# Two-step means and gated weight splits in a two-layer encoder kernel

## The chip, the core and the metric

The kernel runs on one core of a Trainium2 chip. Five engines work side by side, each through its own queue in order: TensorE (PE in the profile; PEld is its weight load), VectorE (DVE), ScalarE (ACT), GpSimd (POOL), and SyncE (SP), which here issues loads. Data comes from memory by DMA into SBUF; TensorE writes into the banks of PSUM. The metric is the time of one execution on the device in microseconds (us), lower is better.

## What is computed

Two layers of an encoder over 256 tokens of width 1024, with a memory of 256 tokens. Cut to what matters here:

```python
for l in range(2):
    x = x + 0.5 * swiglu(rms_norm(x, ffn1_norm[l]), ffn1_w_in[l], ffn1_w_out[l])   # D_FF = 2816
    z = rms_norm(x, mix_norm[l]) @ w_mix_in[l]
    o = [mla_mixer(z..), swa_mixer(z..), na_mixer(z..)]        # three groups of attention heads
    x = x + concat(rms_norm of each group of o) @ w_mix_out[l]
    x = x + mem_xattn(rms_norm(x, mem_norm_x[l]), mem, ...)
    x = x + 0.5 * swiglu(rms_norm(x, ffn2_norm[l]), ffn2_w_in[l], ffn2_w_out[l])
    x = rms_norm(x, block_norm[l])

def mem_xattn(h, mem, mem_g, w_q, w_kv, q_gain, k_gain, w_o):
    m = rms_norm(mem, mem_g)
    q = rms_norm((h @ w_q).reshape(B, S, 4, 64), q_gain)
    kv = (m @ w_kv).reshape(B, M, 2, 4, 64)
    k = rms_norm(kv[:, :, 0], k_gain);  v = kv[:, :, 1]
    p = softmax(einsum('bshd,bmhd->bhsm', q, k) * 64**-0.5)
    return einsum('bhsm,bmhd->bshd', p, v).reshape(B, S, 256) @ w_o
```

All of it is in float32. `rms_norm` divides by the root of the mean square over the last axis, and `swiglu` is `(silu(g) * u) @ w_out` with `g, u` the halves of `x @ w_in`.

## The kernel before

`x` lies transposed, as eight tiles of 128 features x 256 tokens. Each product of two float32 matrices is made of three matmuls (`mm3`, L171): both sides are split into a rounded high part and the rest, and high x high, high x low and low x high are added up in PSUM.

**Weights.** They come as 332 pieces of 128 x 1024 or less in the order of use (`weight_plan`, L43). For each piece `emit_split` (L131) issues a load on SP's queue into one of four `raw` buffers, a cast to `whi` on ScalarE (L142) and a subtraction to `wlo` on VectorE (L145). So the load of a piece waits for the split of the piece four ahead of it. `piece` (L156) hands out a piece and has those up to three ahead split (`ahead`, L151). In layer 0 pieces 94 and 95 are `wq`, 96 and 97 the values' weights `kvv`, 98 and 99 `wo`, 100 and following `f2i`.

**Order.** The engines' queues are filled by a scheduler that reorders within data dependences by a model of time; `tc.issue_after(x)` keeps an instruction behind `x`, and `state["gate"]` (L144) does that for the subtraction of a split.

**Norms.** `Normed` (L187) makes high and low parts of `x` times a gain, squares, and running sums of the squares; the factor 1/rms is multiplied in later. `stats` (L250) takes the mean by two small matmuls per sum of squares (one for each 128 tokens; the trace records each twice), adds EPS on VectorE, and has GpSimd take the root (`rsqrt`, L177). The norm at the end of layer 0 and the one that opens layer 1 are taken together: that `Normed` (`n10`) has two kinds of sums (`pre`), and `stats` writes four columns of `n10ps` behind each other. Other names: `n0`, `n20`, `n21` open the FFNs `f01` (layer 0, first), `f02`, `f12`; `nx0`, `nx1` the mixers; `nm0`, `nm1` the memory attentions.

**FFN** (`ffn`, L295). 22 columns j of the hidden layer, each a gate and an up part of eight `mm3`; columns 0 and 1 are computed together from four banks (`f11s` in `f11`), those from 2 on as `f11i`. `stats` is called behind column 2, `bcast` (L277, `n10pb`: two transposes of the factor) in column 3, and from there VectorE and ScalarE evacuate the columns. Then eight output tiles of 22 `mm3` (`f11o`). `mc` is the first product of the mixer behind it.

**Memory attention** (`mem_attn`, L905). TensorE computes the queries `me0wq` (`formb`), then values of the memory (`kv0kvv`, 16 `mm3` in stretches of 4, 9 and 3) to fill the time in which the head factors are made: `nm0ps` to `nm0m` (mean), `me0e`, `me0m` (with the heads' squares `me0hs`), the root `me0f` on GpSimd, and `me0qn`, the normed queries. `me0pt` transposes them; ScalarE and VectorE copy a half each to `me0qT`. `attend` (L498) goes through four heads: `sc` scores, `ng` the negated maximum, `p` the exponential, `pt` and `pT` its transpose and copies, `pv` values; `finish` divides by the sum (`rc`, `me0o`). `me0ot` transposes the result, and `project` multiplies it with `wo` and adds it into `x` (`gx`), from which `n20h` and `n20l` are made for `f02s`. In layer 1 the names have a 1 (`me1qn`).

## Time and profile before

| | us |
|---|---|
| median of 3 runs (lowest, highest) | 1054.6 (1054.37, 1056.76) |
| the profiled execution | 1054.34 |
| its span, first to last instruction | 1052.6 |
| TensorE busy | 1026.4 |
| VectorE, ScalarE, GpSimd busy | 725.8, 556.7, 68.7 |

The profile is of one execution. Its times are in us from the first instruction. Ends of matmuls are modelled, so that the pace of matmuls is read from their starts or from their count in a window. In a timeline a row may stand for several instructions (x8), and idle time ahead of it stands in brackets with what ended it.

### The profile page before, as it was taken

The numbers are of one execution on the slowest core, as the hardware profiler recorded it, in microseconds if no ns is written. First come the engines' busy times: TensorE is split into PE (matmuls) and PEld (weight loads), VectorE is DVE, ScalarE is ACT, GpSimd is POOL, SyncE is SP. The second block draws the span as 40 slices with busy tenths as digits, with TensorE's granted clock in tenths as the row PEclk, the third lists the DMA queues.
The fourth block names the chain that finished last, engine by engine and source line by source line (L and its number), as shares of the span: only waits on it lengthen the run. The fifth ranks groups of instructions, "written<-read, shape, count | busy, mean of one in ns | idle before, by whom it ended". The sixth has DMA issues, their size and how long they took to land.

```text
span 1052.6 us, 20896 instructions
## 1 busy us (share of the span) xinstructions
PE 1026.4 (98%) x8480; PEld 1005.2 (95%) x8480; DVE 725.8 (69%) x1299; ACT 556.7 (53%) x928; POOL 68.7 (7%) x72
## 2 busy tenths in 40 slices
PE   9999999999997999999999999999999799999996
PEld 8999999988996999999999999999889789999996
DVE  7866677788775876666757666667886768877651
ACT  6745555666553665555545444546674546544541
POOL 1000000361001000000000000002500000000000
PEclk9999999999998999999999999999999999999998
DMA  8866665654022565566555555656631307766641
GB/s 274 281 199 199 187 211 183 198 192 150 17 97 89 197 223 196 189 197 197 190 185 191 181 185 191 205 171 174 226 108 46 124 33 259 206 196 196 190 137 41
DMA packets 54673, 181.79 MB, mean 173 GB/s; under 512 B 6064, under 2 KB 9264, under 8 KB 54576
## 3 DMA queue, kind: packets, MB, share of 16 engines
q1 hardware_dynamic: 53856, 179.33, 53.5%
q8 instruction: 66, 1.08, 0.4%
q10 hardware_dynamic: 720, 1.12, 0.3%
q14 instruction: 31, 0.25, 0.1%
HBM read 179.38 MB, written 1.05 MB: 171 GB/s over the span
## 4 chain that ended last, share of the span: by engine, by line
PE 92%; DVE 2%; POOL 1%; DMA 1%; ACT 1%; issue 1%; SPq 0%; POOLq 0%; DVEq 0%; ACTq 0%
PE f11i L174 4%; PE f11i L172 4%; PE f11i L173 4%; PE f12i L172 3%; PE f01i L173 3%; PE f02i L172 3%; PE f02i L173 3%; PE f01i L172 3%; PE f02i L174 3%; PE f12i L174 3%; PE f12i L173 3%; PE f01i L174 3%; PE f11o L174 2%; PE f11o L172 2%; PE f11o L173 2%; PE f12o L172 2%
## 5 line engine op out<-in xcount | busy, mean ns | idle before, releaser
L145 DVE TENSOR_TENSOR wlo<-raw,whi 128x1024 fp32r<-128x1024 f32 (+4 forms) x337 | 402.6, 1200 | 201.4 <-ACT whi L142 200.0
L142 ACT CAST whi<-raw 128x1024 fp32r<-128x1024 f32 (+4 forms) x337 | 343.8, 1024 | 342.0 <-issue 98.3
L172 PE MATMUL f11i<-n10h,whi 128*128 128x256 f32 x320 | 90.1, 282 | 0.0
L173 PE MATMUL f11i<-n10l,whi 128*128 128x256 f32 x320 | 89.8, 281 | 0.0
L174 PE MATMUL f11i<-n10h,wlo 128*128 128x256 f32 x320 | 89.8, 281 | 0.0
L172 PE MATMUL f01i<-n0h,whi 128*128 128x256 f32 x320 | 88.6, 277 | 0.0
L172 PE MATMUL f02i<-n20h,whi 128*128 128x256 f32 x320 | 88.5, 276 | 0.0
L172 PE MATMUL f12i<-n21h,whi 128*128 128x256 f32 x320 | 88.5, 276 | 0.0
L174 PE MATMUL f02i<-n20h,wlo 128*128 128x256 f32 x320 | 88.5, 276 | 0.0
L174 PE MATMUL f12i<-n21h,wlo 128*128 128x256 f32 x320 | 88.5, 276 | 0.0
L173 PE MATMUL f01i<-n0l,whi 128*128 128x256 f32 x320 | 88.4, 276 | 0.0
L173 PE MATMUL f02i<-n20l,whi 128*128 128x256 f32 x320 | 88.4, 276 | 0.0
L173 PE MATMUL f12i<-n21l,whi 128*128 128x256 f32 x320 | 88.4, 276 | 0.0
L174 PE MATMUL f01i<-n0h,wlo 128*128 128x256 f32 x320 | 88.2, 276 | 0.0
L173 PEld LDWEIGHTS f11i<-n10l,whi 128*128 128x128 f32 x320 | 61.4, 192 | 0.0
L174 PEld LDWEIGHTS f02i<-n20h,wlo 128*128 128x128 f32 x320 | 60.1, 188 | 0.0
L174 PEld LDWEIGHTS f12i<-n21h,wlo 128*128 128x128 f32 x320 | 60.1, 188 | 0.0
L173 PEld LDWEIGHTS f01i<-n0l,whi 128*128 128x128 f32 x320 | 60.1, 188 | 0.0
L172 PEld LDWEIGHTS f11i<-n10h,whi 128*128 128x128 f32 x320 | 60.1, 188 | 0.0
L173 PEld LDWEIGHTS f02i<-n20l,whi 128*128 128x128 f32 x320 | 60.1, 188 | 0.0
L173 PEld LDWEIGHTS f12i<-n21l,whi 128*128 128x128 f32 x320 | 60.1, 188 | 0.0
L172 PEld LDWEIGHTS f01i<-n0h,whi 128*128 128x128 f32 x320 | 60.1, 188 | 0.0
(1026 smaller groups left out, 2916.7 us busy)
## 6 DMA issues: line engine op xcount, KB each, us to landing
raw<-in_w SPq DMA_DIRECT2D x311, 512.0 KB, 4.3
raw<-in_w SPq DMA_DIRECT2D x12, 384.0 KB, 3.5
raw<-in_w SPq DMA_DIRECT2D x8, 416.0 KB, 3.2
kv0mt<-in_mem SPq DMA_DIRECT2D x8, 128.0 KB, 4.3
kv1mt<-in_mem SPq DMA_DIRECT2D x8, 128.0 KB, 3.4
gx<-in_gx SPq DMA_DIRECT2D x2, 256.0 KB, 6.1
gx<-in_gx ACTq DMA_DIRECT2D x1, 323.0 KB, 3.9
raw<-in_w SPq DMA_DIRECT2D x2, 128.0 KB, 4.0
```

The costliest lines, as they stand in the source:

```text
L142: ins = nc.scalar.copy(hi[:, a:b], r[:, a:b])
L145: sub = nc.vector.tensor_tensor(lo[:, a:b], r[:, a:b], hi[:, a:b].bitcast(F32), ALU.subtract)
L172: nc.tensor.matmul(ps, ah, bh, start=first, stop=False)
L173: nc.tensor.matmul(ps, ah, bl, start=False, stop=False)
L174: return nc.tensor.matmul(ps, al, bh, start=False, stop=last)
```

## The change

`mean(n)` is cut out of `stats`: it takes the mean of one kind of sum, and allocates the PSUM tile and makes `m` with the first. A `Normed` with two kinds has the first mean taken behind column 1 of the FFN and the second with `stats` behind column 2. In the memory attention a limit is set on how many pieces are split: four from the first piece of `wq`. Then `one_piece` admits one piece at a time, at four places, and gates its subtraction behind an instruction of VectorE there: behind `me0m`, behind the half of `me0qT`, and at two steps of `attend` behind the copies `pT` or the maximum. The gate of the next is the low part of the attention's result (`me0ol`).

```diff
-    state = {"split": 0, "cur": 0, "tiles": {}, "gate": None}
+    state = {"split": 0, "cur": 0, "tiles": {}, "gate": None, "limit": len(plan)}
...
     def ahead(n):
-        while state["split"] < min(len(plan), n):
+        while state["split"] < min(state["limit"], n):
...
+        def mean(self, n):
+
+            self.total()
+            if n == 0:
+                self.ps = acc(self.name + "ps")
+            v = self.sums[n]
+            for t in range(2):
...
+            if n == 0:
+                self.m = mp.tile([P, 2], F32, tag="r", name=self.name + "m")
+                nc.vector.tensor_scalar(self.m, self.ps[:, 0:2], EPS, None, ALU.add)
+
         def stats(self, r=None):
...
+            self.mean(0 if self.pre is None else 1)
...
             held.append((j, pg, pu))
+            if j == 1 and nx.pre is not None:
+                nx.mean(0)
             if j == 2:
                 nx.stats()
...
-                nc.vector.tensor_reduce(ng, sc, AX.X, ALU.max, negate=True)
+                state["place"] = nc.vector.tensor_reduce(ng, sc, AX.X, ALU.max, negate=True)
...
-            nc.vector.tensor_copy(self.pT[:, 1, :], ps[:, T : 2 * T])
+            state["place"] = nc.vector.tensor_copy(self.pT[:, 1, :], ps[:, T : 2 * T])
...
-        nc.vector.scalar_tensor_tensor(t3(m), t3(hs), 1.0 / dim, bc(e, n), ALU.mult, ALU.add)
+        state["place"] = nc.vector.scalar_tensor_tensor(t3(m), t3(hs), 1.0 / dim, bc(e, n), ALU.mult, ALU.add)
...
+    def one_piece():
+
+        state["gate"], state["limit"] = state["place"], state["limit"] + 1
+        ahead(state["limit"])
+        state["gate"] = None
+
     def mem_attn(l, nx, mem, nxt):
         nm = f"me{l}"
+
+        state["limit"] = state["cur"] + 4
         ps = formb(nm, "wq", 256, 4, nx.h, nx.l)
...
             nx.stats()
-            state["gate"] = None
...
         f = head_factors(nm, hs, 4, 64, e)
+
+        one_piece()
...
-        nc.vector.tensor_scalar(qT[:, 1], pt[:, T:], gq, None, ALU.mult)
+        state["place"] = nc.vector.tensor_scalar(qT[:, 1], pt[:, T:], gq, None, ALU.mult)
+        one_piece()
...
-            nc.vector.tensor_tensor(ol[:, c, :], pt[:, 0:T], oh[:, c, :].bitcast(F32), ALU.subtract)
-
-        attend(heads, {AT["wturn0"]: [lambda: out_transposed(0)]}, AT["e1"], AT["e2"])
+            state["gate"] = nc.vector.tensor_tensor(ol[:, c, :], pt[:, 0:T], oh[:, c, :].bitcast(F32), ALU.subtract)
+
+        hooks = {AT["wturn0"]: [lambda: out_transposed(0)]}
+        hooks[3] = hooks[5] = [one_piece]
+        attend(heads, hooks, AT["e1"], AT["e2"])
+        state["limit"] = len(plan)
```

VectorE's queue before, from the split of piece 97 on in layer 0's memory attention (the number behind `wlo` is the piece):

```order
L145 TENSOR_TENSOR wlo97_3999<-raw97_3996,whi97_3998 128x1024
L145 TENSOR_TENSOR wlo98_4029<-raw98_4026,whi98_4028 128x1024
L145 TENSOR_TENSOR wlo99_4059<-raw99_4056,whi99_4058 128x1024
L145 TENSOR_TENSOR wlo100_4065<-raw100_4062,whi100_4064 128x1024
L263 TENSOR_SCALAR nm0m_4084<-nm0ps_4081 128x2
L528 TENSOR_SCALAR me0e_4086<-nm0m_4084 128x2
L145 TENSOR_TENSOR wlo101_4255<-raw101_4252,whi101_4254 128x1024
L522 SCALAR_TENSOR_TENSOR me0m_4095<-me0hs_4088,me0e_4086 128x8
L145 TENSOR_TENSOR wlo102_4299<-raw102_4296,whi102_4298 128x1024
L919 TENSOR_TENSOR me0qn_4099<-me0wq0_3994,me0f_4096 128x256
L919 TENSOR_TENSOR me0qn_4099<-me0wq1_3995,me0f_4096 128x256
L935 TENSOR_SCALAR me0qT_4148<-me0pt_4133,me0gq_4102 128x256
```

and in the changed kernel:

```order
L145 TENSOR_TENSOR wlo97_3999<-raw97_3996,whi97_3998 128x1024
L265 TENSOR_SCALAR nm0m_4066<-nm0ps_4063 128x2
L539 TENSOR_SCALAR me0e_4068<-nm0m_4066 128x2
L533 SCALAR_TENSOR_TENSOR me0m_4077<-me0hs_4070,me0e_4068 128x8
L145 TENSOR_TENSOR wlo98_4084<-raw98_4081,whi98_4083 128x1024
L939 TENSOR_TENSOR me0qn_4087<-me0wq0_3994,me0f_4078 128x256
L939 TENSOR_TENSOR me0qn_4087<-me0wq1_3995,me0f_4078 128x256
L955 TENSOR_SCALAR me0qT_4136<-me0pt_4121,me0gq_4090 128x256
L145 TENSOR_TENSOR wlo99_4142<-raw99_4139,whi99_4141 128x1024
L469 TENSOR_REDUCE me0a00ng_4151<-me0a00sc_4148 128x2
```

The splits of pieces 98 to 102, which stood ahead of `me0qn`, are behind `me0m` (98), behind `me0qT` (99) and further on. VectorE's queue before, in the middle of the attention, from the second head's copies to the division:

```order
L484 COPY me0a01pT_4199<-me0a01pt_4194 128x256
L485 COPY me0a01pT_4199<-me0a01pt_4194 128x256
L484 COPY me0a10pT_4207<-me0a10pt_4202 128x256
L485 COPY me0a10pT_4207<-me0a10pt_4202 128x256
L484 COPY me0a11pT_4220<-me0a11pt_4215 128x256
L485 COPY me0a11pT_4220<-me0a11pt_4215 128x256
L432 RECIPROCAL me0a0rc_4227<-me0a0pv_4210 128x4
L434 TENSOR_TENSOR me0o_4151<-me0a0pv_4210,me0a0rc_4227 128x2x64 x2
L432 RECIPROCAL me0a1rc_4240<-me0a1pv_4231 128x4
```

and in the changed kernel:

```order
L495 COPY me0a01pT_4193<-me0a01pt_4188 128x256
L496 COPY me0a01pT_4193<-me0a01pt_4188 128x256
L145 TENSOR_TENSOR wlo100_4199<-raw100_4196,whi100_4198 128x1024
L495 COPY me0a10pT_4207<-me0a10pt_4202 128x256
L496 COPY me0a10pT_4207<-me0a10pt_4202 128x256
L495 COPY me0a11pT_4220<-me0a11pt_4215 128x256
L496 COPY me0a11pT_4220<-me0a11pt_4215 128x256
L145 TENSOR_TENSOR wlo101_4234<-raw101_4231,whi101_4233 128x1024
L443 RECIPROCAL me0a0rc_4227<-me0a0pv_4210 128x4
L443 RECIPROCAL me0a1rc_4246<-me0a1pv_4237 128x4
L445 TENSOR_TENSOR me0o_4145<-me0a0pv_4210,me0a0rc_4227 128x2x64 x2
L445 TENSOR_TENSOR me0o_4145<-me0a1pv_4237,me0a1rc_4246 128x2x64 x2
```

The splits of pieces 100 and 101 stand between the copies and ahead of the reciprocals, and the second reciprocal is ahead of the first product. The split of piece 102 comes behind the two `me0ol`, ahead of the first sum into `gx`. Layer 1 has the same order. TensorE's queue before, at the mean matmuls of `n10` behind column 2 of `f11`:

```order
L172 MATMUL f11i2_6796<-n10h_5912,whi171_6738 128x256
L173 MATMUL f11i2_6796<-n10l_5913,whi171_6738 128x256
L174 MATMUL f11i2_6796<-n10h_5912,wlo171_6739 128x256
L258 MATMUL n10ps_6861<-cmean_87,n10s_6282 128x1 x2
L258 MATMUL n10ps_6861<-cmean_87,n10s_6286 128x1 x2
L172 MATMUL f11i3_6874<-n10h_5912,whi172_6768 128x256
L173 MATMUL f11i3_6874<-n10l_5913,whi172_6768 128x256
L174 MATMUL f11i3_6874<-n10h_5912,wlo172_6769 128x256
```

and in the changed kernel, at the first of two places, behind column 1:

```order
L336 MATMUL f11s2_6674<-n10l_5913,whi169_6678 128x256
L336 MATMUL f11s3_6675<-n10l_5913,whi169_6678 128x256
L259 MATMUL n10ps_6800<-cmean_87,n10s_6282 128x1 x2
L172 MATMUL f11i2_6805<-n10h_5912,whi170_6708 128x256
L173 MATMUL f11i2_6805<-n10l_5913,whi170_6708 128x256
L174 MATMUL f11i2_6805<-n10h_5912,wlo170_6709 128x256
```

and at the second, behind column 2:

```order
L172 MATMUL f11i2_6805<-n10h_5912,whi171_6738 128x256
L173 MATMUL f11i2_6805<-n10l_5913,whi171_6738 128x256
L174 MATMUL f11i2_6805<-n10h_5912,wlo171_6739 128x256
L259 MATMUL n10ps_6800<-cmean_87,n10s_6286 128x1 x2
L172 MATMUL f11i3_6874<-n10h_5912,whi172_6768 128x256
L173 MATMUL f11i3_6874<-n10l_5913,whi172_6768 128x256
L174 MATMUL f11i3_6874<-n10h_5912,wlo172_6769 128x256
```

One group of four small matmuls became two groups of two, 48 matmuls of column 2 apart. The two transposes `n10pb0` stand two matmuls earlier than before, inside a weight piece's triple. ScalarE's queue has one change for each layer: the cast of piece 102 stands behind `me0qT` instead of ahead of it. The queues of GpSimd and SP keep their order.

## Rows read from the trace of the kernel before

**Rows 1.** The page, part 1: busy time, share of the span, instructions.

```profile
PE 1026.4 (98%) x8480; PEld 1005.2 (95%) x8480; DVE 725.8 (69%) x1299; ACT 556.7 (53%) x928; POOL 68.7 (7%) x72
```

**Rows 2.** Waits of TensorE (PE): engine, line, waited for: total us, times, longest.

```profile
PE me0pt L930 <- DVE me0qn L919: 7.5, 1, 7.5
PE me1pt L930 <- DVE me1qn L919: 6.0, 1, 6.0
```

**Rows 3.** Timeline of VectorE (DVE), layer 0's memory attention: start, us, instruction [idle before].

```profile
310.32 4.62 DVE L145 TENSOR_TENSOR wlo<-raw,whi 128x1024 fp32r<-128x1024 f32 x4
314.87 0.15 DVE L263 TENSOR_SCALAR nm0m<-nm0ps 128x2 f32<-128x2 f32 x1
318.31 0.16 DVE L522 SCALAR_TENSOR_TENSOR me0m<-me0hs,me0e 128x8 f32<-128x8 f32 x1
321.23 0.76 DVE L919 TENSOR_TENSOR me0qn<-me0wq,me0f 128x256 f32<-128x256 f32 x2 [1.56 <-POOL me0f L178]
326.77 0.69 DVE L458 TENSOR_REDUCE me0a00ng<-me0a00sc 128x2 f32<-128x512 f32 x1 [2.73 <-PE me0a01sc L455]
```

**Rows 4.** Timeline of TensorE, the mean matmuls of layer 0's memory attention.

```profile
310.46 0.61 PE L258 MATMUL nm0ps<-cmean,nm0s 128*128 128x1 f32 x4
```

**Rows 5.** Timeline of ScalarE (ACT), the cast of piece 101, and layer 1's.

```profile
316.09 1.04 ACT L142 CAST whi<-raw 128x1024 fp32r<-128x1024 f32 x1 [1.57 <-DMA raw<-in_w]
...
837.35 1.04 ACT L142 CAST whi<-raw 128x1024 fp32r<-128x1024 f32 x1 [0.87 <-DMA raw<-in_w]
```

**Rows 6.** Timeline of GpSimd (POOL), the root of the head factors, both layers.

```profile
318.55 2.65 POOL L178 TENSOR_TENSOR me0f<-me0m,nhalf 128x8 f32<-128x8 f32 x1 [33.35 <-DVE me0m L522]
...
839.82 1.67 POOL L178 TENSOR_TENSOR me1f<-me1m,nhalf 128x8 f32<-128x8 f32 x1 [32.75 <-DVE me1m L522]
```

**Rows 7.** Table by window, behind the wait: busy (count) by engine, granted clock, DMA.

```profile
core 0: us, PE busy (x) PEld busy (x) DVE busy (x) ACT busy (x) POOL busy (x), PEclk, DMA share, GB/s
321.70:324.80 3.10, 3.09 (x14) 2.71 (x14) 0.77 (x2) 0.47 (x1) 0.00 (x0) 0.50 0.47 178
```

**Rows 8.** The same table, five windows of the FFNs `f01`, `f02`, `f11`.

```profile
12.50:20.50 8.00, 8.00 (x70) 8.00 (x69) 7.30 (x14) 5.77 (x10) 0.00 (x0) 1.00 0.86 285
345.00:355.00 10.00, 10.00 (x87) 10.00 (x86) 9.38 (x17) 6.53 (x13) 0.00 (x0) 1.00 0.36 114
370.00:470.00 100.00, 100.00 (x884) 100.00 (x884) 68.02 (x100) 52.05 (x78) 0.00 (x0) 1.00 0.61 201
526.00:536.00 10.00, 10.00 (x91) 10.00 (x90) 4.91 (x4) 3.44 (x5) 0.00 (x0) 1.00 0.62 204
550.00:650.00 100.00, 100.00 (x851) 100.00 (x851) 67.53 (x103) 48.94 (x74) 0.00 (x0) 1.00 0.57 187
```

**Rows 9.** Timeline of VectorE, layer 1's memory attention.

```profile
832.30 4.62 DVE L145 TENSOR_TENSOR wlo<-raw,whi 128x1024 fp32r<-128x1024 f32 x4
841.74 0.75 DVE L919 TENSOR_TENSOR me1qn<-me1wq,me1f 128x256 f32<-128x256 f32 x2
846.46 0.69 DVE L458 TENSOR_REDUCE me1a00ng<-me1a00sc 128x2 f32<-128x512 f32 x1 [1.92 <-PE me1a01sc L455]
852.64 0.18 DVE L432 RECIPROCAL me1a0rc<-me1a0pv 128x4 f32<-128x4 f32 x1
852.93 0.49 DVE L434 TENSOR_TENSOR me1o<-me1a0pv,me1a0rc 128x128 f32<-128x128 f32 x2
```

**Rows 10.** Timeline of TensorE, layer 1's memory attention.

```profile
845.30 0.48 PE L455 MATMUL me1a00sc<-memkT,me1qT 64*128 64x256 f32 x1
854.23 0.39 PE L949 MATMUL me1ot<-ident,me1o 128*128 128x128 f32 x2
855.13 0.62 PE L172 MATMUL me1wo<-me1oh,whi 128*128 128x256 f32 x3 [0.52 <-ACT me1oh L950]
```

**Rows 11.** Timeline of TensorE, start of layer 0's second FFN (`f02s`).

```profile
342.44 1.07 PE L327 MATMUL f02s<-n20h,wlo 128*128 128x256 f32 x8
343.35 1.12 PE L327 MATMUL f02s<-n20l,whi 128*128 128x256 f32 x8
```

More of the change, by code (lines that the diff above doesn't have):

```diff
@@ L248, in total @@
             return self.sums[-1][0][-1]
-        def stats(self, r=None):
-            self.total()
-            ps = acc(self.name + "ps")
-            for n, v in enumerate(self.sums):
-                for t in range(2):
-                    s = slice(t * P, (t + 1) * P)
-                    for m, q in enumerate(v):
-                        nc.tensor.matmul(
-                            ps[:, 2 * n + t : 2 * n + t + 1], q[0][:, s], cmean[:, 0:1],
-                            start=m == 0, stop=m == len(v) - 1,
-                        )
-            self.m = mp.tile([P, 2], F32, tag="r", name=self.name + "m")
-            nc.vector.tensor_scalar(self.m, ps[:, 0:2], EPS, None, ALU.add)
+        def mean(self, n):
[4 more added lines that the diff above has]
+            for t in range(2):
+                s = slice(t * P, (t + 1) * P)
+                for m, q in enumerate(v):
+                    nc.tensor.matmul(
+                        self.ps[:, 2 * n + t : 2 * n + t + 1], q[0][:, s], cmean[:, 0:1],
+                        start=m == 0, stop=m == len(v) - 1,
+                    )
+            if n == 0:
+                self.m = mp.tile([P, 2], F32, tag="r", name=self.name + "m")
+                nc.vector.tensor_scalar(self.m, self.ps[:, 0:2], EPS, None, ALU.add)
+        def stats(self, r=None):
+            self.mean(0 if self.pre is None else 1)
             if self.factor:
@@ L271, in stats @@
             m2 = small(2, self.name + "m2")
-            nc.vector.scalar_tensor_tensor(m2, self.m, EPS, ps[:, 2:4], ALU.mult, ALU.add)
+            nc.vector.scalar_tensor_tensor(m2, self.m, EPS, self.ps[:, 2:4], ALU.mult, ALU.add)
             self.r0 = mp.tile([P, 2], F32, tag="r", name=self.name + "r0")
```

## The prediction

> **What bounds the kernel now.** I first read the busy line of the page: TensorE (PE) is busy for 98% of the span [rows 1]. So nothing gains but a shorter wait of TensorE, or matmuls that follow each other faster. The waits view names only two waits of TensorE above 1.5 us, one in the memory attention of each layer, 7.5 and 6.0 us, both for `qn`, the normed queries that VectorE (DVE) writes [rows 2]. Then the timeline of DVE shows why `qn` is late [rows 3]. The mean `nm0ps` is on TensorE at 310.46 and takes 0.61 us [rows 4], so DVE could read it at 311.1. But four splits of weight pieces (`wlo`, 4.62 us) stand ahead of its first reader, which starts at 314.87; the fifth split waits for ScalarE, which waits for a load [rows 5], and `me0m` comes only at 318.31. GpSimd's root follows for 2.65 us [rows 6] and `qn` starts at 321.23. During the wait the clock fell: right behind it the granted clock is 0.50, the lower level of 1.2 GHz [rows 7].
>
> The second thing is the pace of the matmuls in the FFNs. All have 256 columns. I take the pace as (window + 0.28 us, since matmuls stick out at its edges) / count. In `f02i` it is 100.28/884 = 113.4 ns, in `f11i` 100.28/851 = 117.8 ns, both at a granted clock of 1.00 [rows 8]. So there is a quick and a slow pace, 4.4 ns apart. The switches stand at the mean matmuls: `f01` is slow ahead of `n0ps` (8.28/70 = 118 ns), `f02` slow ahead of `n20ps` (10.28/87 = 118) and quick behind it, `f11` quick ahead of `n10ps` (10.28/91 = 113) and slow behind it [rows 8]; `f12` repeats `f02`.
>
> **The change: the gates of the memory attention.** In layer 0 one split (piece 97) now stands ahead of `nm0m`, instead of four. It starts at 310.32 as before [rows 3]; with 4.62/4 = 1.15 us each, `nm0m` can start at 311.5. `me0e` and `me0m` follow directly, about 0.18 us later each (an estimate from the 0.15 to 0.17 us that such instructions take [rows 3]), so `me0m` is at 311.85. The root starts 0.24 us behind it as now (318.31 to 318.55 [rows 3, 6]), takes 2.65 us, and `qn` starts at 311.85 + 0.24 + 2.65 + 0.03 = 314.77 instead of 321.23: **6.46 us** earlier. The split of piece 98, gated behind `me0m`, lies under the root. TensorE's work ends at about 321.7 - 7.5 = 314.2 and the transposes come 0.48 us behind `qn`, so some 1.0 us of wait stays.
>
> In layer 1 the first split starts at 832.30 [rows 9]; `nm1m` 833.45, `me1m` 833.8, root 834.05 to 835.72 (1.67 us [rows 6]), `qn` 835.75 instead of 841.74: **5.99 us**, and the wait all but goes (842.2 - 6.0 = 836.2 is where TensorE's work ends).
>
> Behind the transposes the clock matters. After a wait of 1.0 us or none I take it to stay at 1.00; now that stretch runs at 0.50 [rows 7]. What that gives is bounded by nothing and by half of the 3.1 us stretch plus, in layer 0, the scores. It isn't all to be had: ScalarE has the cast of piece 101 ahead of its copy `qT`, and that cast waits for a load whose issue hangs on the first split, which does not move. It starts at 316.09 and takes 1.04 us [rows 5], so `qT` is at 317.1 and its end at 317.6. From the first score to the first reduction it takes 846.46 - 845.30 = 1.16 us at full clock [rows 9, 10]; the split of piece 99, now ahead of that reduction, adds some 0.3. So the reduction is at about 319.0, where the 6.46 us alone would give 326.77 - 6.46 = 320.3: **1.3 us** more in layer 0 (0 to 2.0). In layer 1 the cast runs from 837.35 to 838.4, `qT` to 838.9, the reduction at 840.0 to 840.4 against 846.46 - 5.99 = 840.5 [rows 5, 9]: **0.3 us** (0 to 1.0).
>
> The price: pieces 100 and 101 are split in the middle of the attention, the one ahead of the last two heads' copies, the other ahead of the reciprocal. Two splits are 2.3 us; DVE waits little there (some 0.15 us), so the reciprocal goes from 852.64 to about 854.8. The second reciprocal is now ahead of the first product too (0.2 us), so the product that starts at 852.93 ends near 855.7, and the transposes at 854.23 become 855.7 [rows 9, 10]. The projection behind them (855.13) is **1.5 us** later, in each layer; bounds 0.3 (they fit into gaps) and 2.3. The split of piece 102, between `ol` and the first sum into `x`, costs nothing: TensorE has the whole projection there, and if that cover failed it would be 1.15 us. Loads for later pieces are issued later on SP's queue, since a load waits for the split of the piece four ahead of it; with 24 matmuls a piece, piece 103 is needed 72 x 113.4 ns = 8 us after `f02s` starts, so I price that at nothing, and at 1 us if one piece is late.
>
> Sum: layer 0 -6.46 - 1.3 + 1.5 = -6.3; layer 1 -5.99 - 0.3 + 1.5 = -4.8. Together **-11.1 us**.
>
> **The change: the means in two steps.** The work is the same, four mean matmuls, which the trace records as x8 in one group; now two groups of x4. No engine is waited for there in either place, and the root behind them isn't on the path. What can change is the pace. Three groups of x4 came in at the slow pace and left at the quick one (`n0ps`, `n20ps`, and `n21ps`, which repeats `n20ps`). The new first group comes in at the quick pace; what it leaves is not shown, since the only x4 groups that came in quick (`nm0ps`, `nm1ps`) did so behind a wait of their own. But if it leaves the quick pace, the second one meets the same case and leaves it too; if it leaves the slow one, the second is the case seen three times, slow to quick. Either way `f11` runs quick from there, if the pair of transposes `n10pb` keeps the pace, as the pairs in the other three FFNs do. Matmuls from there to the end of `mc` in layer 1: 19 columns x 48 = 912, `f11o` 8 x 66 = 528, `mc` 72, together 1512 x 4.4 ns = 6.7 us; if column 2 runs slow it costs 48 x 4.4 ns = 0.2. So **-6.4 us**; bounds +0.2 and -6.7.
>
> [...]
>
> **Sum.** The profiled execution took 1054.34 us around its span of 1052.6. 1054.34 - 11.1 - 6.4 = 1036.8. The median shown is 0.26 above the profiled execution: **1037.1 us**. Its own bounds: 1033.5 (1.2 us less for each tail, 0.7 more for each clock term) to 1040.5 (0.8 more for each tail, no clock gain).
>
> **Rivals.** *The pace stays slow* (0.28). The single group of x8 came in quick and left slow, and the pairs `n10pb0` and `n10pb1` left it so; the new `n10pb0` stands inside a weight piece, where the quick FFNs have theirs between two pieces. If the pace belongs to what stands around the matmuls there, the split means bring +0.2: 1037.1 + 6.6 = 1043.7 us. [...]
>
> *DVE and ScalarE take the place of the wait* (0.08): both inserted splits lie fully on the path (+0.8 per layer) and the casts of 1.04 us delay `qT` and the first exponential by one each (+1.04 per layer): +3.7, 1040.8 us.
>
> *The pace turns the wrong way* (0.06), the one that ends slower. `f02s` starts quick and turns slow where it waits for `n20l`: its eight matmuls at 343.35 take 1.12 instead of 1.07 us [rows 11]; only so does `n20ps` come in slow and leave quick. If the moved splits take that wait of 0.05 us away, `f02s` stays quick and `n20ps` may turn it slow, up to the end of `f11s` (912 + 528 + 96 = 1536 matmuls), and likewise `f12` to the end (1440): 2976 x 4.4 ns = 13.1 us, less 1.1 for the quick rest of both `f02s` and `f12s`. `f11` then comes in slow, is quick for one column, and slow again: nothing gained. 1054.6 - 11.1 + 12.0 = 1055.5 us. It decides from the point where `n20l` is in time. Against it: the split of piece 102 ends before the sums into `x`, so the chain from there to `n20l` stays as it is.
>
> *The change doesn't do what it says* (0.02): something else holds `nm0m`, and nothing moves: 1054.6. The order above speaks against it.
>
> **How the numbers follow.** Forecast 0.56, slow pace 0.28, DVE and ScalarE 0.08, wrong way 0.06, nothing 0.02. The range must reach the slow pace at 1043.7 and the low bound of the forecast: 1034.0 to 1044.8. A measurement tells this kernel from no change at about 0.3%, 3.2 us. Faster by more: 0.56 + 0.28 + 0.08 = 0.92. The wrong way ends near no change: 0.04 of it within 0.3%, with the 0.02 of nothing 0.06; the other 0.02, where less is gained in the attention, slower.
>
> **What would show it.** Right: TensorE's waits for `qn` are about 1 us in layer 0 and near nothing in layer 1, with the granted clock 1.00 behind them; the projection's first matmul comes some 11 (layer 0: 6.3) us earlier; `f11i` has as many matmuls in 100 us as `f02i`. Wrong: a new wait of TensorE for the scores, for `me0ot` above 2 us, or for weights in `f02s`; `f11i` still at 851 in 100 us; `f02i` falling to 851.

## The result and the profile after

The changed kernel takes 1038.4 us (median of four runs, 1036.07 to 1039.62) beside 1054.7 us of the kernel before (four runs, 1054.37 to 1056.76) on the same chip: a ratio of 0.984, 95% interval 0.9815 to 0.9863. The forecast was 1037.1 us in a range of 1034.0 to 1044.8. The profiled execution of the changed kernel took 1039.5 us, 14.8 less than that of before, with a span of 1037.7.

TensorE still bounds the kernel; the share is the same 98% of a shorter span (page, part 1), and 6.0 us of its busy time are gone [rows 1]:

```profile
PE 1020.4 (98%) x8480; PEld 998.7 (96%) x8480; DVE 724.9 (70%) x1299; ACT 556.0 (54%) x928; POOL 67.9 (7%) x72
```

The waits of TensorE for `qn`, 7.5 and 6.0 us [rows 2], are 1.0 us each (waits of the changed kernel: engine, line, waited for, total us, times, longest). Behind them stand others, none above 0.8 us: those for the division (`me0o`, `me1o`) and for `qT` are new, that for the exponential (`me0a00p`) was 0.4 us before, and that for `oh` was 0.5 us before as well:

```profile
PE me0pt L950 <- DVE me0qn L939: 1.0, 1, 1.0
PE me1pt L950 <- DVE me1qn L939: 1.0, 1, 1.0
PE me0a00pt L493 <- ACT me0a00p L482: 0.8, 1, 0.8
PE me0a00sc L466 <- ACT me0qT L954: 0.7, 1, 0.7
PE me0ot L970 <- DVE me0o L445: 0.7, 1, 0.7
PE me1ot L970 <- DVE me1o L445: 0.7, 1, 0.7
PE me0wo L172 <- ACT me0oh L971: 0.5, 1, 0.5
```

VectorE's timeline in layer 0's memory attention answers to [rows 3]. `qn` is 6.53 us earlier (321.23 to 314.70) and the first reduction 7.43 us (326.77 to 319.34). The splits of pieces 100 and 101, 1.22 us each, stand at 323.94 and 326.40, and the reciprocal comes only at 327.53, with no idle time ahead of any of them:

```profile
314.70 0.76 DVE L939 TENSOR_TENSOR me0qn<-me0wq,me0f 128x256 f32<-128x256 f32 x2 [1.56 <-POOL me0f L178]
...
319.34 0.68 DVE L469 TENSOR_REDUCE me0a00ng<-me0a00sc 128x2 f32<-128x512 f32 x1
...
323.94 1.22 DVE L145 TENSOR_TENSOR wlo<-raw,whi 128x1024 fp32r<-128x1024 f32 x1
...
326.40 1.22 DVE L145 TENSOR_TENSOR wlo<-raw,whi 128x1024 fp32r<-128x1024 f32 x1
327.53 0.18 DVE L443 RECIPROCAL me0a0rc<-me0a0pv 128x4 f32<-128x4 f32 x1
```

On TensorE, the projection's first matmul and the first of `f02s`, first in the kernel before, then in the changed one (timeline: start, us). The projection comes 6.14 us earlier, `f02s` only 4.63: 1.51 us are lost inside the projection.

```profile
335.45 0.75 PE L172 MATMUL me0wo<-me0oh,whi 128*128 128x256 f32 x4 [0.52 <-ACT me0oh L950]
...
341.52 1.09 PE L327 MATMUL f02s<-n20h,whi 128*128 128x256 f32 x8
```

```profile
329.31 1.15 PE L172 MATMUL me0wo<-me0oh,whi 128*128 128x256 f32 x6 [0.52 <-ACT me0oh L971]
...
336.89 1.09 PE L336 MATMUL f02s<-n20h,whi 128*128 128x256 f32 x8
...
338.73 1.13 PE L336 MATMUL f02s<-n20l,whi 128*128 128x256 f32 x8
```

The table by window (columns as in [rows 7]) says why. The same 50 matmuls (the projection's 48 and two transposes) took 6.1 us at a granted clock of 1.00 before, and 7.5 us at 0.77 now (first fence: before; second: the changed kernel). Inside it the clock is 0.50, 1.2 GHz, for some 3.5 us in layer 0 (third fence, first row) and as long in layer 1 (second row):

```profile
335.40:341.50 6.10, 6.05 (x50) 6.05 (x51) 2.81 (x10) 1.40 (x3) 0.00 (x0) 1.00 0.01 3
```

```profile
329.30:336.80 7.50, 7.49 (x50) 7.49 (x51) 3.84 (x9) 1.40 (x3) 0.00 (x0) 0.77 0.36 128
```

```profile
330.00:333.00 3.00, 3.00 (x16) 3.00 (x15) 1.56 (x2) 0.38 (x1) 0.00 (x0) 0.50 0.14 56
839.00:841.00 2.00, 2.00 (x10) 2.00 (x11) 0.27 (x1) 0.03 (x1) 0.00 (x0) 0.50 0.56 223
```

The means did what was forecast. In `f11i` there are 884 matmuls in 100 us (last row), where there were 851 [rows 8]. `f02` ahead of `n20ps` now runs quick (first row: 10.78/95 = 113.5 ns), behind it, in column 2, slow (second row: 5.28/45 = 117 ns), and quick behind the transposes `n20pb` (third row):

```profile
340.00:350.50 10.50, 10.50 (x95) 10.50 (x94) 9.88 (x18) 6.90 (x13) 0.00 (x0) 1.00 0.40 115
351.50:356.50 5.00, 5.00 (x45) 5.00 (x44) 2.92 (x4) 2.12 (x3) 0.70 (x1) 1.00 0.90 312
364.00:464.00 100.00, 100.00 (x885) 100.00 (x884) 68.52 (x101) 53.14 (x81) 0.00 (x0) 1.00 0.64 200
...
540.00:640.00 100.00, 100.00 (x884) 100.00 (x884) 69.98 (x109) 52.51 (x81) 0.00 (x0) 1.00 0.59 192
```

Layer 1's memory attention begins with `me1wq`, at 825.4 us before and 814.0 us now, 11.4 us earlier (the instructions of the tile, with their first and last start; before, then now):

```profile
L545 PE MATMUL me1wq<-whi,nm1h x16: 276/276/278, 825.4 to 830.3; 128*128 128x256 f32 x16
```

```profile
L556 PE MATMUL me1wq<-whi,nm1h x16: 275/276/277, 814.0 to 819.0; 128*128 128x256 f32 x16
```

From there, VectorE's and TensorE's timelines of the changed kernel: `qn` is 16.40 us earlier than before [rows 9], 5.0 of it gained here; the reduction 17.58, 6.2 gained here; the projection 16.27 [rows 10], 4.9 gained here. ScalarE's timeline (last fence) has the cast of piece 101 and, right behind it, its half of `qT`:

```profile
825.34 0.76 DVE L939 TENSOR_TENSOR me1qn<-me1wq,me1f 128x256 f32<-128x256 f32 x2 [1.56 <-POOL me1f L178]
...
828.88 0.68 DVE L469 TENSOR_REDUCE me1a00ng<-me1a00sc 128x2 f32<-128x512 f32 x1
```

```profile
838.86 1.65 PE L172 MATMUL me1wo<-me1oh,whi 128*128 128x256 f32 x6 [0.52 <-ACT me1oh L971]
...
846.30 1.09 PE L336 MATMUL f12s<-n21h,whi 128*128 128x256 f32 x8
```

```profile
825.89 1.05 ACT L142 CAST whi<-raw 128x1024 fp32r<-128x1024 f32 x1 [0.74 <-DMA raw<-in_w]
826.84 0.47 ACT L954 ACTIVATE me1qT<-me1pt,me1gq 128x256 f32<-128x256 f32 x1
```

GpSimd's root, which took 2.65 us in layer 0 and 1.67 us in layer 1 [rows 6], takes 2.6 us in both, with the split of piece 98 started on VectorE 0.16 us ahead of it in layer 0 (third fence):

```profile
312.09 2.58 POOL L178 TENSOR_TENSOR me0f<-me0m,nhalf 128x8 f32<-128x8 f32 x1 [26.91 <-DVE me0m L533]
```

```profile
822.74 2.57 POOL L178 TENSOR_TENSOR me1f<-me1m,nhalf 128x8 f32<-128x8 f32 x1 [27.01 <-DVE me1m L533]
```

```profile
311.93 1.22 DVE L145 TENSOR_TENSOR wlo<-raw,whi 128x1024 fp32r<-128x1024 f32 x1
```

### The profile page after: what moved, and what is told of

Its sections match the earlier page's. It is cut to its first block, busy times and chain, and to the rows that moved or that the text cites. A ratio compares the mean times of both kernels' runs of the same rounds, so it can differ in the third digit from the quotient of the medians.

```text
span 1037.7 us, 20893 instructions
## 1 busy us (share of the span) xinstructions
PE 1020.4 (98%) x8480; PEld 998.7 (96%) x8480; DVE 724.9 (70%) x1299; ACT 556.0 (54%) x928; POOL 67.9 (7%) x72
## 3 DMA queue, kind: packets, MB, share of 16 engines
q10 hardware_dynamic: 720, 1.12, 0.3%
## 4 chain that ended last, share of the span: by engine, by line
PE 90%; DVE 4%; DMA 2%; issue 1%; POOL 1%; ACT 1%; POOLq 0%; DVEq 0%; ACTq 0%; SPq 0%
PE f11i L172 4%; PE f02i L173 4%; PE f12i L172 4%; PE f01i L173 4%; PE f02i L174 4%; PE f12i L174 4%; PE f12i L173 4%; PE f01i L172 4%; PE f01i L174 3%; PE f11i L174 3%; PE f11i L173 3%; PE f02i L172 3%; PE f12o L173 2%; PE f11o L172 2%; PE f02o L173 2%; PE f02o L174 2%
## 5 line engine op out<-in xcount | busy, mean ns | idle before, releaser
L172 PEld LDWEIGHTS f12i<-n21h,whi 128*128 128x128 f32 x320 | 60.2, 188 | 0.0
L172 PEld LDWEIGHTS f02i<-n20h,whi 128*128 128x128 f32 x320 | 60.2, 188 | 0.0
L174 PEld LDWEIGHTS f11i<-n10h,wlo 128*128 128x128 f32 x320 | 60.1, 188 | 0.0
```

What stands on the lines that cost most here:

```text
L172: nc.tensor.matmul(ps, ah, bh, start=first, stop=False)
L174: return nc.tensor.matmul(ps, al, bh, start=False, stop=last)
```

## The experiments

Four questions: are the two parts of the change independent; what turns the pace of the matmuls; what brings the clock down in the projection; and why `qn` of layer 1 came 1.0 us short.

### The two parts alone

**The means alone** (`e1_means`): the four mean matmuls in two steps, the memory attention as before.

```diff
     def one_piece():
-        state["gate"], state["limit"] = state["place"], state["limit"] + 1
-        ahead(state["limit"])
-        state["gate"] = None
+        pass
...
-        state["limit"] = state["cur"] + 4
...
             nx.stats()
+            state["gate"] = None
...
-        hooks[3] = hooks[5] = [one_piece]
```

> The kernel before with the two-step means alone; the weight splits stay where they were. Theory (each group of mean matmuls turns the pace of the matmuls behind it): f11 runs slow for column 2 only and quick from the second group on, f11i has 884 matmuls in 100 us instead of 851, and the time is 6.4 us under the kernel before, 1048.2. Rival (the quick pace of f11 in the changed kernel comes from what the gates did upstream, for instance the pace at which f02 ends): f11i stays at 851, the time within 0.5 us of 1054.6.

It took 1047.7 us beside 1053.9, a ratio of 0.9938 (0.9921 to 0.9954): 6.2 us, where the theory had 6.4. Its wait for `qn` is as long as before, and the pace in `f11i` is quick (waits, and table by window, 884 in 100 us):

```profile
PE me0pt L949 <- DVE me0qn L938: 7.7, 1, 7.7
```

```profile
550.00:650.00 100.00, 100.00 (x884) 100.00 (x884) 68.98 (x105) 51.32 (x77) 0.00 (x0) 1.00 0.57 192
```

**The gates alone** (`e2_gates`): the changed kernel with the means in one group behind column 2.

```diff
         def mean(self, n):
...
-            v = self.sums[n]
+            for n, v in enumerate(self.sums):
...
-            self.mean(0 if self.pre is None else 1)
+            self.mean(0)
...
-            if j == 1 and nx.pre is not None:
-                nx.mean(0)
```

> The changed kernel with one group of eight mean matmuls behind column 2 as before: the gates alone. Theory (the two parts are independent; the clock falls to 1.2 GHz in the projection of both layers, as in the profile of the changed kernel, where f02s starts 4.6 us and f12s 3.5 us earlier by the gates): 8.1 us under the kernel before and 0.7 more for the quick f02s and f12s, 1045.8; up to 3 us less in an execution in which the clock stays up. f11i at 851 in 100 us. Rival (the parts need each other, the group of eight now leaves the quick pace because the gates changed the state before it): f11i at 884 and 1038 to 1040.

It took 1046.3 us beside 1053.9, 0.9925 (0.991 to 0.9939): 7.6 us, near the 8.8 that the theory took from the changed kernel's profile. `f11i` runs slow behind the group of eight:

```profile
540.00:640.00 100.00, 100.00 (x852) 100.00 (x851) 67.94 (x105) 50.18 (x78) 0.00 (x0) 1.00 0.54 185
```

So the parts are independent within the noise: the quick pace of `f11` needs nothing from the gates, and the gates don't bring it. Their sum, 13.9 us, lies 2.4 under the 16.3 us by which the changed kernel was ahead, and 1.0 under the 14.9 us when it ran once more (below), with intervals of 1.5 to 2.5 us to either side of each of the four; and the profile of `e2_gates` lost more in the projection of layer 1 than that of the changed kernel (8.7 us for its matmuls at a mean granted clock of 0.64, where the changed kernel took 7.3).

### What turns the pace

**All eight behind column 1** (`e3_eight_col1`):

```diff
         def mean(self, n):
...
-            v = self.sums[n]
+            for n, v in enumerate(self.sums):
...
-            self.mean(0 if self.pre is None else 1)
+            if self.pre is None:
+                self.mean(0)
```

So the call behind column 1 writes all four columns of `n10ps`, and `stats` none.

> The changed kernel with all eight mean matmuls in one group behind column 1. Theory (it is the number of groups that decides: each turns the pace once, whatever its size, so one group that comes in quick leaves slow): f11i at 851 in 100 us, 6.7 us slower than the changed kernel, about 1045. Rival (the place decides: behind column 1 the pace recovers where behind column 2 it doesn't): f11i at 884 and the time of the changed kernel, 1038.4.

It took 1046.3 us (two executions, 1044.91 and 1047.73) beside 1053.9, 0.9926 (0.9906 to 0.9946), and `f11i` is slow. So it isn't the place behind column 1.

```profile
540.00:640.00 100.00, 100.00 (x851) 100.00 (x851) 67.82 (x104) 49.58 (x77) 0.00 (x0) 1.00 0.56 186
```

**The first four in the middle of column 2** (`e4_four_half`), 24 matmuls ahead of the second four instead of 48:

```diff
+                    if j == 2 and ps is pg and nx.pre is not None:
+                        nx.mean(0)
...
-            if j == 1 and nx.pre is not None:
-                nx.mean(0)
```

> The changed kernel with the first group of four mean matmuls in the middle of column 2 (behind its gate half) instead of behind column 1: 24 matmuls apart instead of 48. Theory (each group turns the pace, wherever it stands): 24 matmuls slow between the groups, quick behind the second, f11i at 884 in 100 us, the time of the changed kernel, 1038.4 within its spread of 1036 to 1040. Rival (the first must stand behind column 1, between two kinds of accumulation): f11i at 851 and 1045.

It took 1040.0 us (two executions, 1039.97 and 1040.1) beside 1054.2, 0.9867 (0.9842 to 0.9891), with `f11i` quick:

```profile
540.00:640.00 100.00, 100.00 (x885) 100.00 (x884) 70.25 (x108) 52.45 (x81) 0.00 (x0) 1.00 0.60 193
```

**A third group of four** (`e7_third`), behind column 6; its result is read by nothing.

```diff
+            if j == 6 and nx.pre is not None:
+                three = acc(nm + "three")
+                for t in range(2):
+                    for m, q in enumerate(nx.sums[0]):
+                        nc.tensor.matmul(
+                            three[:, t : t + 1], q[0][:, t * P : (t + 1) * P], cmean[:, 0:1],
+                            start=m == 0, stop=m == len(nx.sums[0]) - 1,
+                        )
```

> The changed kernel with a third group of four mean matmuls of no use behind column 6 of f11 (result read by nothing). Theory (each group turns the pace): f11 runs slow from there to the end of mc, 15 columns x 48 + 528 + 72 = 1320 matmuls x 4.4 ns = 5.8 us more, about 1044.2; f11i at 851 in 100 us behind column 6 and quick ahead of it. Rival (the second group brings a lasting quick pace, or the pace belongs to the place): 884 throughout, 1038.4.

It took 1044.05 us (two executions, 1042.9 and 1045.19) beside 1054.2, 0.9905 (0.9877 to 0.9933), where the theory had 1044.2. Ahead of the third group, which stands at 556.3 us, `f11` runs quick (12.28/109 = 112.7 ns), behind it slow (100.28/852 = 117.7 ns):

```profile
539.00:551.00 12.00, 12.00 (x109) 12.00 (x108) 9.87 (x20) 7.30 (x14) 0.00 (x0) 1.00 0.50 178
570.00:670.00 100.00, 100.00 (x852) 100.00 (x851) 63.01 (x90) 48.14 (x71) 0.00 (x0) 1.00 0.55 190
```

So in `f11` one group leaves it slow, two leave it quick, three slow, at each of the places tried (behind columns 1, 2 and 6 and in the middle of 2) and whether a group has four or eight records: each group turns the pace to the other one. What in the chip does that, the runs don't show.

### What brings the clock down in the projection

**No splits in the middle of the attention** (`e5_tail`): 99 and 100 behind `qn`, 101 behind the first `ol`.

```diff
-            nc.vector.tensor_tensor(qn[:, t], hd(ps[t][:, 0:256], 4), bc(f[:, t, :], 64), ALU.mult)
+            state["place"] = nc.vector.tensor_tensor(qn[:, t], hd(ps[t][:, 0:256], 4), bc(f[:, t, :], 64), ALU.mult)
+        qnp = state["place"]
+        one_piece()
+        state["place"] = qnp
+        one_piece()
...
         state["place"] = nc.vector.tensor_scalar(qT[:, 1], pt[:, T:], gq, None, ALU.mult)
-        one_piece()
...
-        hooks[3] = hooks[5] = [one_piece]
```

> The changed kernel with the splits of pieces 99 and 100 behind qn (where VectorE waits 2.35 us for the transposes) and that of 101 behind the first ol, none in the middle of the attention. From the first reduction to the first matmul of the projection it took 8.7 us before and 10.0 us in the changed kernel, and the split of 99 held the reduction 0.36 us; 1.66 us a layer should come back. Theory (the waits of TensorE for the division and for oh, just ahead of the projection, bring the clock down in it): without the 0.7 us wait the granted clock stays 1.00 in the projection, 1.4 to 1.5 us more a layer, so 6.2 us under the changed kernel's profiled 1039.5, about 1033.3. Rival (the low use of TensorE over the whole attention brings it down): the clock is still 0.50 in the projection, and the time is 1036.2.

It took 1033.1 us beside 1053.9, 0.9802 (0.9787 to 0.9817), its four executions within 1.2 us (1032.83 to 1033.98). The granted clock is 1.00 through the projection of both layers, with 50 matmuls in 6.0 us each:

```profile
327.10:333.10 6.00, 5.97 (x50) 5.98 (x51) 4.98 (x11) 1.39 (x3) 0.00 (x0) 1.00 0.47 155
833.90:839.90 6.00, 6.00 (x50) 6.00 (x51) 4.99 (x11) 1.39 (x3) 0.00 (x0) 1.00 0.51 136
```

**The waits filled** (`e6_fill`): the splits stay in the middle, and the division stays late; TensorE gets matmuls of no use in its waits for the division and for `oh`.

```diff
+            def fill(n, behind):
+                with tc.issue_after(behind.ins):
+                    for i in range(n):
+                        ins = nc.tensor.matmul(fp[:, 0:T], nx.h[:, 0, 0:P], nx.h[:, 0, :], start=True, stop=True)
+                return ins
+
+            if c == 0:
+                fp = acc(nm + "fill")
+                before = fill(7, state["pv"])
...
+            if c == 0:
+                state["fill"] = fill(4, turned)
```

> The changed kernel with 11 matmuls of no use in each memory attention, 7 behind the last pv and 4 behind the first transposes ot, in TensorE's waits of 0.70 and 0.52 us ahead of and in the projection; their result is read by nothing. All else, the late division too, stays. Theory (the idle time of TensorE there brings the clock down): granted clock 1.00 through both projections, the 1.5 and 1.4 us that the profile of the changed kernel loses there come back, less 0.1 for each filled wait: every execution near the fastest of the changed kernel, 1036.3, with a spread of about 1 us instead of 3.5. Rival (the low use over the whole attention brings it down): the clock falls to 0.50 in some projections as before, 1036 to 1040 with a median at 1038.4 or above.

It took 1036.6 us beside 1054.2, 0.9833 (0.9814 to 0.9852). The clock stayed at 1.00 in both projections:

```profile
330.60:336.60 6.00, 6.00 (x50) 6.00 (x51) 3.85 (x9) 1.39 (x3) 0.00 (x0) 1.00 0.43 146
838.90:844.90 6.00, 5.97 (x50) 5.97 (x51) 3.84 (x9) 1.39 (x3) 0.00 (x0) 1.00 0.47 144
```

Three of its four executions lie between 1036.25 and 1036.83; the fourth, 1038.44, is the profiled one, which is 1.3 us late already at `nm0ps` (311.7 us, where the changed kernel has it at 310.45), so not by the projection. The mean granted clock of its four executions is 0.996 to 0.997, that of the changed kernel's eight 0.992 to 0.996. The rival, that the low use of the attention is enough by itself, is out: all of it was left as it was, and 11 matmuls in 1.2 us of waits decide. They raise the use of the whole stretch too, though, so the runs don't show whether the idle time must stand just there. Nor is a wait of this length enough: from the end of the values to the projection in layer 0 the changed kernel has waits of 0.96, 0.70, 0.77 and 0.70 us, then that of 0.52, and the clock stays at 1.00 up to the projection, 9 us and more behind the first three (table by window of the changed kernel):

```profile
313.90:329.30 15.40, 11.68 (x82) 9.50 (x81) 10.87 (x25) 6.71 (x14) 0.77 (x1) 1.00 0.38 119
```

**The changed kernel once more** (`e9_after_again`), to see how steady the fall is.

> The changed kernel itself once more, in five rounds beside the next two on the same chip. If the clock falls by chance in the projection of either layer, its executions spread over 1036 to 1040 as before, in steps that answer to one or two projections at 1.2 GHz; a median of about 1038.4. If the first four executions were unusual, the spread is about 1 us as in e5_tail.

It took 1039.5 us beside 1054.4, 0.9852 (0.983 to 0.9874), from 1037.4 to 1040.67, its median 1.1 us above the expected one. In its profile the clock stays at 1.00 through the projection of layer 0 and falls in layer 1 for 7 us (first row), twice as long as in the first profile. It falls there already in the wait for the division, with TensorE idle since 835.9 us (second and third row), ahead of the first `ot` at 836.58 and so ahead of the wait for `oh`:

```profile
835.00:843.50 8.50, 7.28 (x38) 6.74 (x38) 3.90 (x10) 0.74 (x2) 0.00 (x0) 0.60 0.43 121
835.90:836.20 0.30, 0.00 (x0) 0.00 (x0) 0.30 (x3) 0.00 (x0) 0.00 (x0) 1.00 0.74 300
836.30:836.60 0.30, 0.02 (x1) 0.03 (x1) 0.30 (x3) 0.00 (x0) 0.00 (x0) 0.50 0.05 14
```

So the kernel alone doesn't decide the fall. The attention of the changed kernel stands in six profiles, that is in twelve projections (the changed kernel twice, `e2_gates`, `e3_eight_col1`, `e4_four_half`, `e7_third`): the clock fell in ten of them, in three inside the wait for the division, in the others up to 0.8 us behind the projection's first matmul. In the twelve projections of the six profiles without the wait for the division (`e5_tail` and its repetition, `e6_fill`, and the three below) it fell in none. The wait of 0.5 us for `oh` stands in ten of these, and in the four projections of the kernel before and of `e1_means`, where the clock stayed at 1.00 too: alone it takes nothing down. What sets whether, where and for how long the clock falls stays open.

**`e5_tail` once more** (`e10_tail_again`):

> e5_tail once more: 1033.1 with a spread of about 1 us, 5.3 us under the changed kernel on the same chip. If it differed from the changed kernel by the chip it ran on, the difference is under 3 us.

1034.0 us (1033.41 to 1034.44), 0.9802 (0.9782 to 0.9821), on the chip on which the changed kernel took 1039.5: 5.5 us less.

**The cast of piece 101 behind `qT`** (`e8_tail_cast`, and once more as `e11_cast_again`):

```diff
-            ins = nc.scalar.copy(hi[:, a:b], r[:, a:b])
+            with tc.issue_after(state["cast"].ins) if state["cast"] else nullcontext():
+                ins = nc.scalar.copy(hi[:, a:b], r[:, a:b])
...
-        nc.scalar.activation(qT[:, 0], pt[:, 0:T], AF.Copy, scale=gq)
+        state["cast"] = nc.scalar.activation(qT[:, 0], pt[:, 0:T], AF.Copy, scale=gq)
```

> As e5_tail, with ScalarE's cast of piece 101 behind its half of qT instead of ahead of it. In e5_tail the cast starts at 315.81 and qT at 316.77, while its transposes are done at about 315.8, and TensorE waits 0.48 us for qT. Theory (that cast holds the scores): the wait goes, and the scores come 0.4 to 0.9 us earlier in each layer; 0.5 us a layer reaches the projection, so 1.0 us under e5_tail, 1032.1. Rival (both casts, 2.0 us, then stand ahead of memV and of the first exponential, which take up what qT gains): no more than 0.3 us from e5_tail, 1033.1.

> e8_tail_cast once more. Its trace showed layer 0's projection 0.6 us earlier behind nm0ps than e5_tail's and layer 1's no earlier: 0.5 us under e10_tail_again, 1032.6. If the chip made the difference, no difference.

The first took 1032.7 us beside 1054.2, 0.9798 (0.9781 to 0.9814), the second 1032.7 beside 1054.4, 0.9794 (0.9774 to 0.9815). The wait for `qT`, 0.5 us in layer 0 of `e5_tail`, is gone from both. Against `e10_tail_again` on the same chip it is 1.3 us less by the medians, but the executions overlap (1032.33 to 1034.41 against 1033.41 to 1034.44): a small gain is likely and not shown. The 1032.7 lies between the theory's 1032.1 and the rival's 1033.1.

### Why the root got slower

**No split beside the root** (`e12_root_free`): as `e8_tail_cast`, with 98 and 99 behind `qn` and 100 behind the third head's reduction.

```diff
         f = head_factors(nm, hs, 4, 64, e)
-        one_piece()
...
+        def behind_reduction():
+            state["place"], cast, state["cast"] = state["reduced"], state["cast"], None
+            one_piece()
+            state["cast"] = cast
+        hooks[2] = [behind_reduction]
```

> As e8_tail_cast, with no weight split beside GpSimd's root: the splits of 98 and 99 stand behind qn, that of 100 behind the third head's reduction (where VectorE waits 1.14 us), 101 and 102 as there; ScalarE's cast of 102 behind the last exponential. In the kernel before the root took 1.67 us in layer 1 with the split starting 0.78 us behind it, and 2.65 us in layer 0 with the split from its start; in the changed kernel 2.58 us in both, the last 1.56 us of it behind the end of the split. Theory (a split beside the root's start holds the root): the root takes 1.5 to 1.7 us, qn comes 1.0 us earlier, TensorE's waits for qn of 1.0 us all but go, 1.0 us a layer less: 1030.7. Rival (the root takes 2.58 us by itself, and the end at 1.67 us was read wrong): root and qn stay, 1032.7, no change.

It took 1031.3 us (1030.77 to 1033.12) beside 1054.5, 0.9783 (0.9769 to 0.9796), the lowest median of all. The root takes 1.67 us in both layers (timeline of GpSimd), `qn` comes at 313.34 us, and TensorE goes from the values to the transposes of `qn` within 0.3 us (timeline of TensorE); its waits view names `qn` no more:

```profile
311.64 1.67 POOL L181 TENSOR_TENSOR me0f<-me0m,nhalf 128x8 f32<-128x8 f32 x1 [26.91 <-DVE me0m L536]
```

```profile
817.71 1.67 POOL L181 TENSOR_TENSOR me1f<-me1m,nhalf 128x8 f32<-128x8 f32 x1 [27.01 <-DVE me1m L536]
```

```profile
313.50 0.28 PE L177 MATMUL kv0kvv<-whi,kv0l 128*128 128x256 f32 x1
313.82 0.88 PE L956 MATMUL me0pt<-ident,me0qn 128*128 128x128 f32 x4
```

The root is 0.9 us longer when a weight split starts just ahead of it. The span is 1.9 us under that of `e11_cast_again` (1029.0 against 1030.9), the median 1.4, which the intervals of the two ratios don't tell apart. The traces do show the gain: from `nm0ps` to the projection it is 15.78 us against 16.79, in layer 1 15.75 against 16.44.

The Trainium skill, SBUF — State Buffer, section Who interferes with whom, has a rule on this: a VectorE instruction with two SBUF inputs, as `raw` and `whi` of the split are, contends with a GpSimd instruction that reads SBUF, since its second input comes through a shared read interface, and the shared ports are an exclusive lock. The trace agrees where the split starts ahead of the root: in layer 0 of the changed kernel VectorE stands idle for 1.56 us behind the split until the root ends, nearly the root's own 1.67. The other order shows no lock: in layer 1 of the kernel before, a split starts 0.78 us behind the root, when its cast is done, and neither takes longer than alone (1.23 us, VectorE's timeline of the kernel before; the root 1.67 [rows 6]):

```profile
840.60 1.23 DVE L145 TENSOR_TENSOR wlo<-raw,whi 128x1024 fp32r<-128x1024 f32 x1 [0.87 <-ACT whi L142]
```

## Why the prediction was right, and which terms were off

**Where the time went.** By the starts above: 4.6 us were gained up to `f02s` (forecast 6.3), 6.8 from there to `me1wq` (forecast 6.4), 3.5 from there to `f12s`, which began at 861.2 us before (forecast 4.8). Together 14.9, the difference of the spans (forecast 17.5). Of the other executions the fastest, 1036.07 us, is 1.0 under the forecast. By the prediction's own terms its bounds come to 1033.3 and 1040.3, not 1033.5 and 1040.5, and its range begins above the lower of them; nothing hangs on either.

**The gates in layer 0.** Each step held to the projection. `nm0m` moved ahead as worked out; `qn` came 6.53 us earlier (6.46 forecast). The clock term, 1.3 us behind the transposes, was 0.9 (7.43 - 6.53 = 0.90); TensorE does run at full clock there, and the chosen value between 0 and 2.0 was near. The reduction was forecast at 319.0 us, behind the cast, and came at 319.34. The price of the two inserted splits was 1.3 us (7.43 - 6.14 = 1.29; forecast 1.5). The sum to the projection, 6.14, was forecast as 6.3.

**The gates in layer 1.** The sum held, 4.9 for 4.8, but not its first term: `qn` was worked out with the root's 1.67 us of layer 1 [rows 6] and gained 5.0 us instead of 5.99. The step that failed was to take that duration along while the change puts a split beside the root's start in both layers, as it stood in layer 0 of the kernel before; `e12_root_free` shows the price, 0.9 us. It cost nothing up to the reduction (6.2 us gained, 5.99 + 0.3 forecast), since `qn` doesn't set that: as the prediction had it, `qT` starts where the cast of piece 101 ends (826.84 us, the cast from 825.89), and by this timeline an earlier `qn` would have waited there. From the first transpose to the first score it took 1.87 us at a granted clock of 1.00, where it was 3.08 at 0.50: the 1.2 us by which the reduction gained more than `qn` (6.2 - 5.0).

**The projection, the term that was left out.** The prediction priced the late division at what it delays, 1.5 us, and saw in it a wait of TensorE; it let the clock rest there, although it had just read that a wait brings the clock down [rows 2, 7]. The wait of 0.7 us for the division, with the 0.5 us for `oh` behind it, brought it down in ten of twelve projections, and in the profiled execution the projection took 1.5 us more in layer 0 (from its first matmul to `f02s` 7.58 us, 6.07 before) and 1.4 in layer 1 (7.44 against 6.07). `e6_fill` shows that it is idle time of TensorE and not the late division by itself, and `e5_tail` that both prices go with the splits. Together that is 2.9 us, and the profiled execution fell 2.7 short of the forecast (14.8 for 17.5). It is also the likely reason why the changed kernel spreads over 4.6 us where `e5_tail` spreads over 1.6: in each of its two runs the fastest execution is the one with the highest mean granted clock, 0.996.

**The means.** Right in size (6.2 us in `e1_means`, 6.4 forecast) and in the reason by which it was taken: if the first group leaves the quick pace, the second is the case of `n20ps`, slow to quick. That is what happened; column 2 runs slow (36 matmuls from 530 to 534 us, 4.28/36 = 119 ns), the rest quick. The rival of 0.28, a pace that belongs to what stands around the matmuls, falls with the 884 of the changed kernel and of `e1_means`, and `e3_eight_col1`, `e4_four_half` and `e7_third` show what decides instead.

**The pace that turns the wrong way** (0.06). Its first half came true, though not by its reason: the wait for `n20l` is still there (1.13 us for the eight matmuls at 338.73, 1.12 before), and `f02s` stays quick behind it; `n20ps` turns it slow, as the rival said. Why `f02s` stays quick the runs don't show. It was the second half that failed: the transposes `n20pb` 48 matmuls later turn it back, so that it cost 0.2 us and not 13. In the kernel before, `n10pb` came in slow and left slow ([rows 8]: 851 behind them), so nothing in it promised that; the pairs of transposes follow no rule that these runs show.

**Casts and loads.** ScalarE's cast of piece 101 held `qT` as forecast (a wait of TensorE of 0.7 us in layer 0); later loads cost nothing that the waits name.

## What to carry to other kernels

Work that is moved off a critical wait wants a place where its engine is idle, not the nearest place behind: the three splits that `e5_tail` took out of the attention and put behind `qn` and `ol`, where VectorE stood idle, brought 5.5 us on the same chip. A short wait of TensorE costs more than its length when the clock falls in it or behind it, so price the matmuls behind a new wait at half the clock too, and look there first. Where one shape of matmul runs at two paces, count them per window around each interruption; the number of interruptions may decide, and it is cheap to change.

## What the runs showed of the hardware that was not expected

Each group of the small float32 matmuls (four or eight records of one column) in `f11` turned the pace of the 256-column matmuls behind it between 113.4 and 117.8 ns, for 100 us and more: one, two and three groups gave 851, 884 and 852 matmuls in 100 us. Behind an attention of small matmuls, a wait of TensorE of 0.7 us with one of 0.5 us behind it took the granted clock to 0.50 for 3.5 or 7 us, though in two of twelve cases not at all; 11 matmuls of no use in these waits kept it at 1.00. And a small root on GpSimd, 1.67 us by itself, took 2.58 us when a subtraction of two SBUF tensors had started on VectorE just ahead of it; one that started 0.78 us behind it changed nothing.
